# Keys' transposes and first heads one unit later, bias tables ahead of the first product, forget columns in eight pieces

## The chip, the cores and the metric

The kernel runs on one core of a Trainium2 chip. The metric is the time of one execution on the device in microseconds (us), as the median of several runs; the profile shows one execution. The engines are PE (TensorE, matrix products and transposes), DVE (VectorE), ACT (ScalarE), POOL (GpSimd) and SP (SyncE, which here only issues DMAs). Each engine takes its instructions in order.

## The reference, cut to what matters

Two residual layers on x of 256 rows and 1024 columns, all in float32. Each layer normalizes x, multiplies it with one wide input matrix, feeds the columns to two groups of attention heads with a SiLU gate each, and adds the product with an output matrix. The change is in the first layer, with groups A (block-sparse, here plain causal with a linear position bias) and B (forgetting attention).

```python
h = rmsnorm(x, norm_gain[0])
proj = h @ w_in_ab[0]                      # 1024 x 4104
qa, ka, va, ga, qb, kb, vb, gb, fb = split_cols(proj, [512] * 8 + [8])
qa, ka = rmsnorm(heads(qa), moba_q_gain), rmsnorm(heads(ka), moba_k_gain)
s = qa @ ka.T * scale - slope[h] * (t - s) # causal; slope[h] = 2 ** -(h + 1)
ya = softmax(s) @ va
log_f = log_sigmoid(fb + b_forget)         # the last 8 columns, one per head
s = qb @ kb.T * scale + cumsum(log_f)[t] - cumsum(log_f)[s]
yb = softmax(s) @ vb
x = x + concat(ya * silu(ga), yb * silu(gb)) @ w_out_ab[0]
```

## The kernel before, in words

Weights come in tiles of 512 KB. A tile is loaded by SP into one of four raw buffers (`wraws`, L108), then split in two: ACT casts the high part (`whi`, L120) and DVE subtracts it from the raw tile to get the low part (`wlo`, L121), into one of five buffers. A product is then three matmuls (`mm3`, L258 to L260). A raw buffer is free again when `wlo` is done; a buffer of the split parts is free when PE has used the tile. `loads` keeps three tiles ahead of PE.

In the first layer tile n is the n-th in order: 0 to 7 are qa and ka together (one block of 128 rows by 1024 columns each), 8 to 11 va, 12 to 15 qb, 16 to 19 kb (256 columns each and rows of 1 KB, with 4 forget columns copied in by POOL at L105 from the tile `wf`), 20 to 23 vb, 24 to 31 the gates, 32 to 39 the output. Tiles 0 to 3 have raw buffers of their own.

PE's order is the order of the text. It goes by units: `tick` runs one unit's matmuls (mostly one tile, 12 matmuls of 512 columns), then one step of each running generator, latest first, and then lets new tiles be loaded. `qk_heads` is such a generator for query or key columns: squares and sums, inverse root by ACT's tables, a Newton step and the scaled copies, two empty steps apart from that, and then PE's transposes (L377) whose results ACT and DVE bring to SBUF with the gains (`kf` L387, `khi` L394, `klo` L395). The keys of the first product start one unit after the queries (`later`) and use a spare buffer (`room=True`). `values` copies the values out of their two PSUM banks (L404). All PSUM tiles share eight banks. `heads_a` computes scores (L477, L481), softmax, transposes of the probabilities (L509) and the product with the values (L551) of four heads; `play(12, {1: [heads_a(0)], 5: [heads_a(1)]})` starts it at units 1 and 5 of the twelve that hold tiles 12 to 23.

Up to `gain_cols(0)` the order on all engines is written out by hand (`manual_schedule`). Behind it only PE's is; the order on the other engines is made by a planner with costs of its own, which may move an instruction ahead of others that are not yet due.

`biases` fills `mask` and the tables `negA` of the eight heads, 128 x 256 each, from `rel`, and `tri`, which the forgetting heads need. The first four tables are written between the first units, the other four behind the hand-ordered part. `wf` is filled by one DMA on POOL's queue.

Of the kernel before, what the change touches and what calls it, by code (L numbers as in the profile page):

```python
# [12 lines left out]
OP = mybir.AluOpType  # L13
# [4 lines left out]
KT = D // 128  # L18
HD = 64
EPS = 1e-6  # L20
BIG = 1e30
# [8 lines left out]
def trunk_kernel(  # L30
# [6 lines left out]
    nc = tc.nc  # L37
    x, out = x[0], out[0]
    w_ab, wo_ab, w_cd, wo_cd = w_in_ab[0], w_out_ab[0], w_in_cd[0], w_out_cd[0]
# [20 lines left out]
    def xload(t):  # L60
        nc.sync.dma_start(xs[:, t, :], x[t * 128:(t + 1) * 128, :])


    rel = cst.tile([128, 256], F32, name="rel")
# [7 lines left out]
    def params(eng, rows):  # L72
        for i in rows:
            g = gains[i]
            eng.dma_start(
                prow[i:i + 1, :].rearrange("o (r d) -> o r d", r=2),
                bass.AP(tensor=g.tensor, offset=g.offset, ap=[[64, 1], [0, 2], [1, 64]]))
# [17 lines left out]
    wf = cst.tile([128, KT, 8], F32, name="wf")  # L95


    def wraws(parts, nk, n, raw=None):
        if raw is None:
            raw = wraw.tile([128, WF], F32, name="raw")  # L100
        rv = raw[:, 0:nk * n].rearrange("p (k n) -> p k n", k=nk)
        for (c0, src) in parts:
            if isinstance(src, tuple):
                k0, f0 = src
                nc.gpsimd.tensor_copy(rv[:, :, c0:c0 + 4], wf[:, k0:k0 + nk, f0:f0 + 4])  # L105
                continue
            m = src.shape[1]
            last["sp"] = nc.sync.dma_start(rv[:, :, c0:c0 + m],  # L108
                                           src.rearrange("(k p) n -> p k n", p=128))
        return raw  # L110

    def wload(parts, nk, n, raw=None, pieces=1):
# [15 lines left out]
    tiles, wt, units, running = [], [], [], []  # L128
# [38 lines left out]
    def rsqrt_tables(m, shape):  # L167
        tag = "x".join(str(n) for n in shape[1:])
        y = sml.tile(shape, F32, name="rs_y" + tag)
        nc.scalar.activation(y, m, AF.Ln)  # L170
        nc.scalar.activation(y, y, AF.Exp, bias=0.0, scale=-0.5)
        return y
# [21 lines left out]
    def x_transp(t, j):  # L194
        ps = pa.tile([128, 4, 128], F32, name="at", tag="ps")
        for i in range(4):
            k = 4 * j + i
            nc.tensor.transpose(ps[:, i, :], xs[:, t, k * 128:(k + 1) * 128], ident)
        return ps
# [139 lines left out]
    def qk_heads(ps, nh, col, dst, dup=False, room=None):  # L339
        m = sml.tile([128, 2, nh], F32, name=f"qk_m{nh}")  # L340
        for t in range(2):
            sq = scr.tile([128, 512], F32, name="sq", bufs=3)
            nc.scalar.activation(sq[:, 0:nh * HD], ps[t][:, 0:nh * HD], AF.Square)
            nc.vector.tensor_reduce(m[:, t, :],  # L344
                                    sq[:, 0:nh * HD].rearrange("p (h d) -> p h d", d=HD),
                                    axis=AX.X, op=OP.add)
            nc.vector.tensor_scalar(m[:, t, :], m[:, t, :], 1.0 / HD, H["em"][:, t:t + 1],
                                    op0=OP.mult, op1=OP.add)
        yield
        y = rsqrt_tables(m, [128, 2, nh])  # L350
        yield
        r = rsqrt_newton(m, y, [128, 2, nh])
        qns = []
        for t in range(2):
            if room is None:
                qn = scr.tile([128, 512], F32, name="qn", bufs=2)
            else:
                if t == 0:
                    spare = scr.tile([128, 4, 384], F32, name="e", bufs=2).rearrange("p h n -> p (h n)")
                qn = spare[:, t * 512:(t + 1) * 512]  # L360
            qns.append(qn)
            src = ps[t][:, 0:nh * HD].rearrange("p (h d) -> p h d", d=HD)
            rr = r[:, t, :, None].to_broadcast([128, nh, HD])
            if dup:
                qd = qn[:, 0:nh * 128].rearrange("p (h u d) -> p h u d", u=2, d=HD)
                for u in range(2):
                    nc.vector.tensor_tensor(out=qd[:, :, u, :], in0=src, in1=rr, op=OP.mult)
            else:
                nc.vector.tensor_tensor(out=qn[:, 0:nh * HD].rearrange("p (h d) -> p h d", d=HD),
                                        in0=src, in1=rr, op=OP.mult)  # L370
        yield
        yield
        npair = nh if dup else nh // 2
        for t in range(2):
            pt = pa.tile([128, 4, 128], F32, name="at", tag="ps")
            for i in range(npair):
                nc.tensor.transpose(pt[:, i, :], qns[t][:, i * 128:(i + 1) * 128], ident)  # L377
            dst(t, pt[:, 0:npair, :], H["pcol"][:, col:col + 1])
# [295 lines left out]
    mask = cst.tile([128, 256], F32, name="mask")  # L674
    tri = scr.tile([128, 512], F32, name="ytmp", bufs=1)[:, 0:256]
    negA = cst.tile([128, 8, 256], F32, name="negA")

    def biases(heads):
        if 0 in heads:
            nc.vector.tensor_scalar(mask, rel, 0.0, BIG, op0=OP.is_lt, op1=OP.mult)  # L680
        else:
            nc.vector.tensor_scalar(tri, rel, 128.0, None, op0=OP.is_le)
        for h in heads:
            nc.vector.scalar_tensor_tensor(out=negA[:, h, :], in0=rel, scalar=2.0 ** -(h + 1),
                                           in1=mask, op0=OP.mult, op1=OP.add)

    def heads_a(half):
        yield from quad64("a", half, lambda i: i, lambda h: h * 64, H["va"],
                          lambda h: negA[:, 4 * half + h, 128:256], lambda h: negA[:, 4 * half + h, :])
# [167 lines left out]
    with tc.manual_schedule():  # L857
        nc.vector.memset(wz, 0.0)
        raws = []
        for n in ("yth", "ytl"):  # L860
            r = act.tile([128, 2, 1024], F32, name=n)
            raws += [r[:, 0, :], r[:, 1, :]]
        xload(0)
        wraws(*tiles[0], raws[0])
        xload(1)
        for i in range(1, 4):
            wraws(*tiles[i], raws[i])
        nc.gpsimd.iota(rel, pattern=[[-1, 256]], base=128, channel_multiplier=1,
                       allow_small_or_imprecise_dtypes=True)
        nc.vector.tensor_scalar(ident, rel[:, 0:128], 128.0, None, op0=OP.is_equal)  # L870
        nc.vector.memset(prow, 0.0)
        params(nc.gpsimd, (0, 4, 1, 5))
        warm(WARM[0])
        pgt = pv.tile([128, 512], F32, name="av", tag="ps")
        nc.tensor.transpose(pgt[:, 0:16], grow, ident[0:16, 0:16])
        nc.vector.tensor_copy(gcol, pgt[:, 0:16])
        p0 = x_transp(0, 0)
        warm(WARM[1])
        h_block(0, 0, 0, p0[:, 0, :])
        h_block(0, 0, 1, p0[:, 1, :])  # L880
        wt.append(wload(*tiles[0], raws[0], 2))
        mm_first(0, 0, 0)
        p1 = x_transp(1, 0)
        h_block(0, 1, 0, p1[:, 0, :])
        h_block(0, 1, 1, p1[:, 1, :])
        mm_first(0, 0, 1)
        wt.append(wload(*tiles[1], raws[1], 2))
        for j in range(2):
            mm_first(0, 1, j)
        for k in (2, 3):  # L890
            h_block(0, 0, k, p0[:, k, :])
            h_block(0, 1, k, p1[:, k, :])
        run_first(1)
        p0, p1 = x_transp(0, 1), x_transp(1, 1)
        wt.append(wload(*tiles[2], raws[2], 2))
        for k in (4, 5):
            h_block(0, 0, k, p0[:, k - 4, :])
            h_block(0, 1, k, p1[:, k - 4, :])
        run_first(2)
        wt.append(wload(*tiles[3], raws[3], 2))  # L900
        for k in (6, 7):
            h_block(0, 0, k, p0[:, k - 4, :])
            h_block(0, 1, k, p1[:, k - 4, :])
        run_first(3)
        at["freed"] += 3
        loads(3)
        bfor = bcast(nc.gpsimd, "bfor", b_forget, 8)
        nc.gpsimd.dma_start(wf, w_ab[:, 4096:4104].rearrange("(k p) n -> p k n", p=128))
        g = norm_r()
        next(g)  # L910
        running.append(g)
        at["freed"] += 1
        tick(1)
        biases((0, 1, 2, 3))
        tick(3)
        gain_cols(0)

    def play(n, starts):
        for i in range(n):
            for g in starts.get(i, ()):  # L920
                running.append(g)
            tick()

    biases(range(4, 8))
    tick(4)
    play(12, {1: [heads_a(0)], 5: [heads_a(1)]})
    play(12, {0: [heads_b(0)], 3: [heads_b(1)]})
    drain()
    tick(4)
# [50 lines left out]
```

## Time and profile before

| what | value |
|---|---|
| median of 3 runs | 278.92 us |
| lowest and highest run | 276.66 and 279.52 us |
| the profiled execution | 279.85 us |
| its span in the profile | 278.1 us |
| busy in the span: PE, DVE, ACT, POOL | 267.6, 212.2, 178.6, 7.2 us |

The span is the time from the first to the last recorded instruction; what the run takes beyond it lies around the program. Busy time of PE counts a matmul as long as the profile models it, at whatever clock it ran.

### The profile page before, as it was taken

To read this page: it belongs to the slowest core of one execution; us is meant where nothing else is said; L and a number is where in the kernel's file an instruction comes from. 1 tells how busy PE (TensorE), PEld (TensorE's weight loads), DVE (VectorE), ACT (ScalarE), POOL (GpSimd) and SP (SyncE) were. 2 spreads that over 40 slices of the span, in tenths; PEclk is the share of its full clock that TensorE was granted. 3 is DMA by queue.
4 is the path that set the end of the run, shared out by engine and by line. 5 is a ranking of instruction groups with operands and counts; after the bars stand their busy time and mean duration, and the time that the engine had idled before them with its cause. 6 is when DMAs were issued, how large, how long until landed. Compare 5 with 4: busy or idle time off the path is not lost.

```text
span 278.1 us, 4629 instructions
## 1 busy us (share of the span) xinstructions
PE 267.6 (96%) x1665; PEld 225.7 (81%) x1665; DVE 212.2 (76%) x499; ACT 178.6 (64%) x394; POOL 7.2 (3%) x15
## 2 busy tenths in 40 slices
PE   7999999779999999999999999999999999999994
PEld 2876788558998889999788888888987899897784
DVE  2667998287877549999954988776999888698822
ACT  3469572576687557699742845465785798898500
POOL 6000003000000000000000000000000000000000
PEclk9999999979999999999999999999999999999999
DMA  7974864671444472205855367665508125307012
GB/s 238 202 317 128 225 194 150 195 239 24 148 143 116 118 222 78 77 8 165 247 195 165 90 213 242 212 181 182 167 1 272 35 73 175 132 4 222 5 75 76
DMA packets 26297, 41.38 MB, mean 149 GB/s; under 512 B 1665, under 2 KB 13330, under 8 KB 26274
## 3 DMA queue, kind: packets, MB, share of 16 engines
q1 hardware_dynamic: 26050, 41.04, 47.7%
q0 software_dynamic: 192, 0.04, 1.4%
q8 instruction: 13, 0.21, 0.3%
q14 instruction: 10, 0.08, 0.1%
q10 hardware_dynamic: 32, 0.01, 0.0%
HBM read 40.03 MB, written 1.05 MB: 148 GB/s over the span
## 4 chain that ended last, share of the span: by engine, by line
PE 74%; DMA 9%; DVE 8%; ACT 5%; issue 1%; SPq 1%; ACTq 0%
PE pj L258 21%; PE pj L259 20%; PE pj L260 20%; DMA ytl<-in_w_in_ab_dram 5%; DMA raw<-in_w_in_ab_dram 4%; DVE wlo L121 4%; PE at L509 3%; PE av L551 3%; ACT whi L120 2%; PE at L481 2%; PE at L377 2%; PE at L477 1%; DVE qk_m L344 1%; ACT yb L235 1%; DVE klo L395 1%
## 5 line engine op out<-in xcount | busy, mean ns | idle before, releaser
L121 DVE TENSOR_TENSOR wlo<-raw,whi 128x1024 fp32r<-128x1024 f32 (+1 forms) x70 | 85.2, 1223 | 21.8 <-ACT whi L120 18.3
L120 ACT CAST whi<-raw 128x1024 fp32r<-128x1024 f32 (+1 forms) x70 | 72.4, 1048 | 38.0 <-PE pj L259 20.4
L258 PE MATMUL pj<-whi,hth 128*128 128x512 f32 (+2 forms) x192 | 73.7, 384 | 0.6 <-ACT whi L120 0.5
L260 PE MATMUL pj<-wlo,hth 128*128 128x512 f32 (+2 forms) x192 | 71.2, 371 | 0.5 <-DVE wlo L121 0.5
L259 PE MATMUL pj<-whi,htl 128*128 128x512 f32 (+2 forms) x192 | 71.1, 370 | 0.0
L258 PEld LDWEIGHTS pj<-whi,hth 128*128 128x128 f32 x192 | 36.7, 191 | 8.5 <-ACT whi L120 2.0
L260 PEld LDWEIGHTS pj<-wlo,hth 128*128 128x128 f32 x192 | 36.6, 191 | 8.1 <-DVE wlo L121 1.6
L259 PEld LDWEIGHTS pj<-whi,htl 128*128 128x128 f32 x192 | 36.9, 192 | 5.6
L258 PE MATMUL pj<-hth,whi 128*128 128x256 f32 x128 | 37.0, 289 | 0.0
L260 PE MATMUL pj<-htl,whi 128*128 128x256 f32 x128 | 36.0, 281 | 0.0
L259 PE MATMUL pj<-hth,wlo 128*128 128x256 f32 x128 | 35.9, 281 | 0.0
L258 PE MATMUL pj<-whi,yth 128*128 128x512 f32 (+1 forms) x68 | 26.4, 388 | 0.0
L260 PE MATMUL pj<-wlo,yth 128*128 128x512 f32 (+1 forms) x68 | 25.9, 381 | 0.0
L259 PE MATMUL pj<-whi,ytl 128*128 128x512 f32 (+1 forms) x68 | 25.8, 380 | 0.0
L258 PEld LDWEIGHTS pj<-hth,whi 128*128 128x128 f32 x128 | 24.1, 188 | 0.7 <-issue 0.3
L259 PEld LDWEIGHTS pj<-hth,wlo 128*128 128x128 f32 x128 | 24.2, 189 | 0.0
L260 PEld LDWEIGHTS pj<-htl,whi 128*128 128x128 f32 x128 | 24.1, 188 | 0.0
L490 ACT ACTIVATE e<-e,mn 128x128 f32<-128x128 f32 x32 | 12.5, 390 | 8.9 <-DVE mn L486 8.9
L492 ACT ACTIVATE e<-e,mn 128x256 f32<-128x256 f32 x32 | 15.8, 495 | 0.0
L258 PEld LDWEIGHTS pj<-whi,yth 128*128 128x128 f32 x68 | 12.8, 188 | 2.7 <-issue 0.3
L260 PEld LDWEIGHTS pj<-wlo,yth 128*128 128x128 f32 x68 | 12.8, 188 | 2.6
L259 PEld LDWEIGHTS pj<-whi,ytl 128*128 128x128 f32 x68 | 12.8, 188 | 2.5
(167 smaller groups left out, 390.0 us busy)
## 6 DMA issues: line engine op xcount, KB each, us to landing
raw<-in_w_in_ab_dram SPq DMA_DIRECT2D x28, 512.0 KB, 7.9
raw<-in_w_in_cd_dram SPq DMA_DIRECT2D x26, 512.0 KB, 4.5
raw<-in_w_out_ab_dram SPq DMA_DIRECT2D x8, 512.0 KB, 3.7
raw<-in_w_out_cd_dram SPq DMA_DIRECT2D x8, 512.0 KB, 4.6
xs<-in_x_dram SPq DMA_DIRECT2D x2, 512.0 KB, 6.0
yth<-in_w_in_ab_dram SPq DMA_DIRECT2D x2, 512.0 KB, 7.0
ytl<-in_w_in_ab_dram SPq DMA_DIRECT2D x2, 512.0 KB, 12.7
out_dram<-xs SPq DMA_DIRECT2D x3, 256.0 KB, 2.0
```

The source lines that it names most:

```text
L120: last["act"] = nc.scalar.copy(hi[:, c], raw[:, c])
L121: last["dve"] = nc.vector.tensor_tensor(out=lo[:, c], in0=raw[:, c], in1=hi[:, c].bitcast(F32), op=OP.subtract)
L235: nc.scalar.activation(dump, xs[:, t, :], AF.Square, accum_out=ss[:, t:t + 1])
L258: nc.tensor.matmul(ps, ah, bh, start=first, stop=False)
L259: nc.tensor.matmul(ps, al, bh, start=False, stop=False)
L260: nc.tensor.matmul(ps, ah, bl, start=False, stop=last)
L377: nc.tensor.transpose(pt[:, i, :], qns[t][:, i * 128:(i + 1) * 128], ident)
L481: nc.tensor.matmul(scs[b][:, 128:384], q[r[b], i, :], k[r[b], ik, :], start=n == 0, stop=n == 2)
L490: nc.scalar.activation(e[:, 0:128], e[:, 0:128], AF.Exp, bias=mn[:, 0:1], scale=-1.0, accum_out=sm[:, 0:1])
L492: nc.scalar.activation(e[:, 128:384], e[:, 128:384], AF.Exp, bias=mn[:, 1:2], scale=-1.0, accum_out=sm[:, 1:2])
L509: nc.tensor.transpose(pt[:, i * 128:(i + 1) * 128], blocks[j + i], ident)
L551: nc.tensor.matmul(av[64 * b:64 * b + 64, i, t * 128:256], v[:, t, c:c + 64], p, start=t == 0, stop=t == 1)
```

## The change

Four edits. The wait before the transposes in `qk_heads` is one step longer for the keys of the first product, and `heads_a` starts at units 2 and 6 in place of 1 and 5. `mask` and tables 0 to 2 are computed right behind `ident` and the clearing of `prow`, tables 3 to 5 behind `gcol`; tables 6 and 7 and `tri` stay behind the hand-ordered part. The forget columns are loaded by eight DMAs on SP's queue, each of 128 rows of 32 bytes, behind the loads of tiles 8 to 15, and the one DMA on POOL's queue is gone.

```diff
@@ wraws
                                            src.rearrange("(k p) n -> p k n", p=128))
+        k = len(wt) - KT
+        if 0 <= k < KT:
+            nc.sync.dma_start(wf[:, k, :], w_ab[k * 128:(k + 1) * 128, 4096:4104])
         return raw
@@ qk_heads
         yield
         yield
+        if room is not None:
+            yield
         npair = nh if dup else nh // 2
@@ biases
     def biases(heads):
-        if 0 in heads:
-            nc.vector.tensor_scalar(mask, rel, 0.0, BIG, op0=OP.is_lt, op1=OP.mult)
-        else:
-            nc.vector.tensor_scalar(tri, rel, 128.0, None, op0=OP.is_le)
         for h in heads:
@@ the part ordered by hand
         nc.vector.memset(prow, 0.0)
+        nc.vector.tensor_scalar(mask, rel, 0.0, BIG, op0=OP.is_lt, op1=OP.mult)
+        biases((0, 1, 2))
         params(nc.gpsimd, (0, 4, 1, 5))
...
         nc.vector.tensor_copy(gcol, pgt[:, 0:16])
+        biases((3, 4, 5))
         p0 = x_transp(0, 0)
...
         bfor = bcast(nc.gpsimd, "bfor", b_forget, 8)
-        nc.gpsimd.dma_start(wf, w_ab[:, 4096:4104].rearrange("(k p) n -> p k n", p=128))
...
         tick(1)
-        biases((0, 1, 2, 3))
         tick(3)
         gain_cols(0)
@@ behind it
-    biases(range(4, 8))
+    biases((6, 7))
+    nc.vector.tensor_scalar(tri, rel, 128.0, None, op0=OP.is_le)
     tick(4)
-    play(12, {1: [heads_a(0)], 5: [heads_a(1)]})
+    play(12, {2: [heads_a(0)], 6: [heads_a(1)]})
```

## Rows read from the trace of the kernel before

**Rows 1.** The page, part 1: busy us, share of the span, instructions.

```profile
PE 267.6 (96%) x1665; PEld 225.7 (81%) x1665; DVE 212.2 (76%) x499; ACT 178.6 (64%) x394; POOL 7.2 (3%) x15
```

**Rows 2.** Timeline of PE, 46 to 70 us: start, length, what, idle before.

```profile
49.56 0.60 PE L377 MATMUL at<-ident,e 128*128 128x128 f32 x4
52.23 0.66 PE L377 MATMUL at<-ident,e 128*128 128x128 f32 x4 [2.07 <-ACT v L404]
...
56.43 0.49 PE L477 MATMUL at<-kf,qf 64*128 64x128 f32 x4 [0.75 <-ACT kf L387]
...
59.80 0.79 PE L258 MATMUL pj<-whi,hth 128*128 128x512 f32 x1
...
63.75 0.39 PE L258 MATMUL pj<-whi,hth 128*128 128x512 f32 x1
```

**Rows 3.** Windows of PE: length, busy (instructions), granted clock, DMA share, GB/s.

```profile
60.00:62.50 2.50, 2.50 (x7) 0.57 0.73 217
```

**Rows 4.** Timeline of ACT, 50 to 56 us.

```profile
50.53 1.06 ACT L120 CAST whi<-raw 128x1040 fp32r<-128x1040 f32 x1 [4.67 <-DMA raw<-in_w_in_ab_dram]
51.50 0.68 ACT L404 ACTIVATE v<-pj,n_r 128x512 f32<-128x512 f32 x1
...
54.73 1.06 ACT L120 CAST whi<-raw 128x1040 fp32r<-128x1040 f32 x1 [1.39 <-DMA raw<-in_w_in_ab_dram]
55.69 0.68 ACT L387 ACTIVATE kf<-at,pcol 128x512 f32<-128x512 f32 x1
```

**Rows 5.** The raw tile's DMAs issued in 43 to 45 us (tile 18).

```profile
L108 SPq DMA_DIRECT2D raw<-in_w_in_ab_dram x1: 762/762/762, 43.9 to 43.9; - x1
...
DMA to landing us min/median/max: 13.0/13.0/13.0
```

**Rows 6.** Windows of DVE: length, busy (instructions), clock, DMA share, GB/s.

```profile
28.00:44.00 16.00, 15.96 (x34) 1.00 0.73 211
```

**Rows 7.** Line L684: duration ns min/median/max, first and last start us.

```profile
L684 DVE SCALAR_TENSOR_TENSOR negA<-rel,mask x8: 415/418/426, 29.3 to 37.0; 128x256 f32<-128x256 f32 x8
```

**Rows 8.** Timeline of all engines, 0 to 33 us.

```profile
3.76 0.17 DVE L876 COPY gcol<-av 128x16 f32<-128x16 f32 x1 [2.00 <-PE av L875]
...
4.70 0.91 POOL L908 DMA_DIRECT2D wf<-in_w_in_ab_dram  x1
...
14.89 1.04 PE L198 MATMUL at<-ident,xs 128*128 128x128 f32 x8
15.36 1.14 ACT L120 CAST whi<-ytl 128x512 fp32r<-128x512 f32 x2 [1.97 <-DMA ytl<-in_w_in_ab_dram]
...
23.23 0.50 PE L260 MATMUL pj<-wlo,hth 128*128 128x512 f32 x1 [0.53 <-DVE wlo L121]
...
29.34 1.43 DVE L684 SCALAR_TENSOR_TENSOR negA<-rel,mask 128x256 f32<-128x256 f32 x4
...
32.54 1.28 ACT L343 ACTIVATE sq<-pj 128x512 f32<-128x512 f32 x2 [1.22 <-PE pj L260]
```

**Rows 9.** DMA issues by line: count, KB, us to landing.

```profile
wf<-in_w_in_ab_dram POOLq DMA_DIRECT2D x1, 32.0 KB, 10.7
...
sink<-in_swa_sinks_dram SPq DMA_DIRECT2D x1, 4.0 KB, 2.5
```

**Rows 10.** Windows: length, PE, PEld, DVE, ACT, POOL, clock, DMA share, GB/s.

```profile
6.00:9.00 3.00, 2.50 (x8) 1.62 (x7) 1.65 (x3) 1.41 (x3) 0.00 (x0) 1.00 1.03 404
...
10.00:11.50 1.50, 1.50 (x6) 1.13 (x5) 0.91 (x3) 1.23 (x3) 0.00 (x0) 1.00 0.00 0
11.50:14.00 2.50, 2.50 (x13) 2.02 (x12) 2.10 (x6) 1.32 (x5) 0.00 (x0) 1.00 0.41 169
...
34.00:44.00 10.00, 10.00 (x44) 7.88 (x43) 10.00 (x24) 6.28 (x11) 2.58 (x3) 1.00 0.70 209
```

**Rows 11.** Timeline of ACT, 60 to 70 us.

```profile
66.53 1.05 ACT L120 CAST whi<-raw 128x1024 fp32r<-128x1024 f32 x1 [0.60 <-PE pj L259]
```

**Rows 12.** Timeline of ACT, 68 to 105 us.

```profile
87.11 1.56 ACT L511 COPY pT<-at 128x512 f32<-128x512 f32 x3
```

## Prediction

> **What bounds the kernel now.** I read the page first: TensorE (PE) is busy for 267.6 of 278.1 us [rows 1], so what can be won is its idle time, some 10 us, and stretches in which it is busy but slow. Then I read PE's timeline forward and looked for gaps and for the granted clock. Between the start and the tail they lie in one stretch, and idle time of VectorE (DVE), ScalarE (ACT) or the queues elsewhere is not worth a look.
>
> That stretch, 49 to 64 us, reads so [rows 2]. Tile 12 of the weights (the first of the four tiles of the forgetting queries) ends at 49.6, then the four transposes of the first half of the first heads' keys run. The other four need a PSUM bank and start at 52.23, 2.07 us late, released by an ACT copy of values. Tile 13 follows until 55.7. Then the scores of the first heads wait 0.75 us for kf, then again for khi and klo, and tile 14 starts at 59.80. It takes until 63.75, 3.95 us, because PE's granted clock had fallen after these stalls: 0.57 of full speed between 60.0 and 62.5, so mostly its lower level of 1.2 GHz out of 2.4 [rows 3]. The tile before it took 55.68 - 52.23 less 0.6 us for four transposes, about 2.9 us, so the clock costs about 1.1.
>
> Who is late is seen on ACT [rows 4]. ACT takes its instructions in order. The cast of tile 16 sits in its queue between the two copies of values, and waited 4.67 us for that tile's DMA, so the second copy, which frees the bank, came at 51.50. The cast of tile 17 sits ahead of kf and waited 1.39 us more for its DMA, so kf began at 55.69. From kf's start to PE's return at 59.80 it is 4.1 us: kf, khi in two pieces, klo in two, two pairs of scores. So the root is in-order ACT behind DMAs that land late. Tile 18 takes 13.0 us from its issue at 43.9, which puts it at 56.9 [rows 5].
>
> These DMAs are issued when a raw buffer comes free, which is when DVE has finished the tile four before. DVE was busy for 15.96 us of the 16 from 28 to 44 [rows 6], and the bias tables are in there.
>
> **Part 1: the tables leave that stretch.** Eight negA instructions ran between 29.3 and 37.0 [rows 7]; four in a row took 1.43 us, so 0.36 each, about 3 us for all [rows 8]. How much of that moves tiles 16 to 18? The squares of the first queries start at 32.54, released by PE [rows 8], so what DVE saves before them waits for PE. The four tables behind them are on the chain: 4 x 0.36 = 1.4 us. I bound the gain for tiles 15 to 18 by 1.0 (some is lost in waits for casts) and 1.4, plus what the start gives. Tables 6 and 7 and tri now stand outside the hand order: if the planner leaves them where they are written, they take back under 1 us of it, hence the lower bound. The six early tables cost DVE 6 x 0.36 + 0.2 = 2.4 us. Three stand in the gap of 2.00 us ahead of gcol, and three in the one behind it, which ends when ACT delivers the first hth [rows 8]. Their price is nothing while x is on its way; without that cover it would be at most the 2.4.
>
> **Part 2: the forget columns.** The one 32 KB DMA on GpSimd's queue was issued at 4.7 us [rows 8] and landed 10.7 us later, at 15.4 [rows 9]. In the same time the weights stood still: 0 GB/s from 10.0 to 11.5 and 169 from 11.5 to 14.0, against 404 before the hole [rows 10]. Counting lost bytes at 400 GB/s, that is 1.5 us + 2.5 x 0.58 = 2.9, with the edges about 3.5 us of the queue. ACT then waited 1.97 us for tile 2, and PE 0.53 us at 23.23 for tile 4's low part [rows 8]. Without the hole tile 2 is there when ACT is free; but ACT's next h blocks need the transposes of x, which PE does from 14.89 to 15.9 in either case, so not all of the 1.97 us is won. Bounds: PE's own 0.53 and ACT's 1.97. I take 0.9, nearer to PE's row, since that is the engine that counts.
>
> What it adds: eight DMAs of 128 rows of 32 bytes on SP's queue, each behind one of tiles 8 to 15 and so ahead of the next tile. SP's issue is cheap and SP waits for buffers anyway. On the rings the price is not in the trace. From above: a DMA of just that shape, the sinks, took 2.5 us from issue to landing [rows 9], 20 us for eight, though most of it is latency. From below: nothing, since the queue was only 0.70 busy from 34 to 44 [rows 10]. In between, the 3.5 us hole over eight pieces, 0.44 each. I take the 0.44, half of it hidden in the free 0.3, which leaves the lower part of the gain: tiles 16 to 18 land 1.0 to 2.2 us earlier (1.0 to 1.4 of part 1, plus 0 to 0.9 of the start, less the pieces). The wait added is GpSimd's: its copies into tiles 16 and 17 now wait for the pieces. Behind them on GpSimd stands nothing else, and the cast of tile 16 waits until 50.5 for its own DMA, so this is hidden by several us.
>
> The Trainium skill speaks against this part. Its page "DMA: Bandwidth & Descriptors", section "Rules for kernel authors", says to merge small transfers, since below 64 KB one pays mostly overhead, and its section "Bandwidth" has a measured 0.68 us for 4 KB against 0.95 for 64 KB. By that, as an estimate, eight pieces would be 5.4 us of queue in place of under 0.95. This trace agrees for small rows in so far as the 32 KB cost the queue 3.5 us; it doesn't show pieces on SP's queue. The rule bears on the slower rival below.
>
> **Part 3: keys' transposes and heads one unit later.** Nothing is added or removed, but PE now runs tile 13 directly behind tile 12 and has it done at about 52.4, or 51.5 with the 0.9 of the start. The bank for the second four transposes is freed by the copy of values: today 52.2, then 50 to 51. So the 2.07 us stall goes. Transposes 1.2 us, then tile 14, 2.9 us: PE stands before the scores at about 55.6 with tile 14 done.
>
> What is late next? The scores still need kf, and the question is which cast stands ahead of kf on ACT. The trace shows the planner's habit: a tile's cast goes just where its buffer comes free, ahead of the activations that end the same unit. Tile 16 stood between the two value copies, tile 17 ahead of kf [rows 4], tile 20 at 66.53, the moment that PE lets go of tile 15 [rows 11]. There are five buffers, so tile 18's buffer is tile 13's. With the transposes now behind tile 13, tile 18 goes ahead of kf as tile 17 did. Then kf starts when tile 18 has landed (56.9 less 1.0 to 2.2, so 54.7 to 55.9) and is cast (1.06): 55.8 to 57.0. Add the 4.1 us: PE resumes at 59.9 to 61.1. Before, the same work was done at 63.75. That gains 2.65 to 3.85. PE idles again for some 3 us in 5, so the clock may fall again; with even odds, half of 1.1.
>
> The later units shift too. The second heads' 12 transposes now come in the same unit as those of the first forgetting keys, so more banks are wanted at once. The three copies that free theirs took 1.56 us [rows 12]; that is the upper bound, and below there is nothing to win. I take 0.2.
>
> **The sum.** Middle 3.3, less 0.55 for the clock, less 0.2: 2.6 us. The profiled execution took 279.85 us (span 278.1 and 1.75 around it) and would take 277.2; it was 0.9 above the median of the runs, so against the median of 278.92 I forecast 276.3. PE's busy share of 96% [rows 1] leaves little slack behind this stretch, so what is won there should reach the end.
>
> **The rivals.**
> Tile 17 and not 18 gates kf. If the planner places tile 18's cast behind khi, kf waits only for tile 17, which is there by about 53.5, cast by 54.6: PE resumes at 57.6 to 58.8, with little idling and no fall of the clock. Gain 4.9 to 6.1: 272.8 to 274.0. For it: tile 18 stood behind khi before. Against: the habit above.
>
> The gain is eaten. The pieces take back what DVE gives, tile 18 lands at 56.9 as before, PE resumes at 62.05 and the clock falls in full: 63.75 - 63.15 = 0.6: 278.3. For it: tile 18's 13.0 us show how slow this queue can be [rows 5]; against: the free share [rows 10].
>
> Slower: the pieces clog SP's queue. They stand ahead of tiles 9 to 16 in the one queue that feeds everything, and ACT takes what lands in order. Break-even is where PE resumes at 63.75 - 1.1, so tile 18 at 57.5: 1.6 to 2.8 us of delay beyond the cover, 0.2 to 0.35 per piece. With 0.44 each and no cover it would be about 1 us slower; with 1 us each, 8 us later than 55.3 (the middle of 54.7 to 55.9), PE resumes at 68.5, with the clock 5.8 slower: 284.7. I price it at 281.5. The free share of the queue speaks against. The rule of the Trainium skill named above points the same way as this rival.
>
> **How the numbers follow.** Forecast 0.51, tile 17 gating 0.20, eaten 0.17, slower 0.12. The measurement can tell about 1%, 2.8 us, from no change, so faster means below 276.1. Of the forecast (own range 275.1 to 278.4) a little under half lies there, with the first rival: 0.44. Same: the rest of the forecast, the eaten gain and the mild end of slower: 0.44. Slower 0.12. The range 272.9 to 279.4 leaves out the top of the first rival and most of the last.
>
> **What the profile would show.** PE without a gap between tile 12 and the end of tile 14. ACT's order: tile 18's cast ahead of kf, waiting for its DMA. DVE's tables before 6 us. No standstill of the weights at 10 us, and ACT's wait for tile 2 gone. Tiles 16 to 18 issued 1 to 2 us earlier. I am wrong if the ACT order differs, if tiles 9 to 18 land later than before, or if a new PE wait shows at the second heads' transposes.

## The result, and the profile after

The changed kernel takes 274.57 us (median of 4 runs, 273.74 to 275.19), against 279.22 for the kernel before in the same comparison. The ratio is 0.9879 with a 95% interval of 0.9838 to 0.9920. That is 1.2% faster, and the interval leaves out no change. One of the four runs of before, 281.04, fell in a slower state, and the ratio goes by the others; without it the median of before is 278.92 and the difference of the medians 4.35 us, where the ratio makes it 3.4. The forecast was 276.3, with a range of 272.9 to 279.4.

The profiled execution took 273.74 us with a span of 271.9, where that of before took 279.85 and 278.1. These 6.2 us of span are more than the 4.35 us between the medians, in part because the two profiles differ in the clock as well; that is taken apart below.

On the page, part 1 answers to [rows 1]: PE's busy time fell by 3.3 us and the span by 6.2.

```profile
span 271.9 us, 4636 instructions
PE 264.3 (97%) x1665; PEld 223.4 (82%) x1665; DVE 212.1 (78%) x499; ACT 178.2 (66%) x394; POOL 6.3 (2%) x14
```

PE's timeline after, for the start and the middle (start, length, what, idle before). It answers to [rows 2] and, in its first two lines, to [rows 8].

```profile
13.96 1.04 PE L201 MATMUL at<-ident,xs 128*128 128x128 f32 x8
21.19 0.50 PE L263 MATMUL pj<-wlo,hth 128*128 128x512 f32 x1
...
50.30 1.04 PE L382 MATMUL at<-ident,e 128*128 128x128 f32 x8
...
54.49 0.49 PE L482 MATMUL at<-kf,qf 64*128 64x128 f32 x4 [0.38 <-ACT kf L392]
55.65 0.39 PE L486 MATMUL at<-khi,qhi 64*128 64x256 f32 x2 [0.67 <-ACT khi L399]
...
56.52 0.38 PE L486 MATMUL at<-klo,qhi 64*128 64x256 f32 x2 [0.36 <-DVE klo L400]
...
57.41 0.50 PE L261 MATMUL pj<-whi,hth 128*128 128x512 f32 x1
...
82.73 1.47 PE L514 MATMUL at<-ident,e 128*128 128x128 f32 x12
```

The reader is to see four things. The low part of tile 4 starts 2.04 us earlier (21.19 for 23.23) and no longer waits. The eight transposes of the keys run in one piece without the stall of 2.07 us. The waits at the scores are still there: 0.38, 0.67 and 0.36 us. And at 57.41 PE starts tile 15, which began at 63.75 before: 6.34 us earlier, about as much as the whole span won (6.2). So nearly all that happened lies ahead of this point.

ACT's timeline after, in the same two stretches; it answers to [rows 8] and [rows 4].

```profile
12.91 1.13 ACT L123 CAST whi<-ytl 128x512 fp32r<-128x512 f32 x2
14.59 1.59 ACT L224 ACTIVATE hth<-at,gcol 128x128 fp32r<-128x128 f32 x4 [0.55 <-PE at L201]
...
18.84 1.98 ACT L123 CAST whi<-raw 128x1024 fp32r<-128x1024 f32 x2
...
46.13 1.06 ACT L123 CAST whi<-raw 128x1040 fp32r<-128x1040 f32 x1 [2.77 <-DMA raw<-in_w_in_ab_dram]
47.09 0.68 ACT L409 ACTIVATE v<-pj,n_r 128x512 f32<-128x512 f32 x1
...
49.80 1.06 ACT L123 CAST whi<-raw 128x1040 fp32r<-128x1040 f32 x1 [0.87 <-DMA raw<-in_w_in_ab_dram]
52.80 1.06 ACT L123 CAST whi<-raw 128x1040 fp32r<-128x1040 f32 x1 [1.93 <-DMA raw<-in_w_in_ab_dram]
53.76 0.68 ACT L392 ACTIVATE kf<-at,pcol 128x512 f32<-128x512 f32 x1
```

The cast of tile 2 at 12.91 waits for no DMA, where it waited 1.97 us; behind it ACT waits 0.55 us for PE's transposes of x. The cast of tile 16 runs at 46.13 and so the copy of values behind it at 47.09, 4.4 us earlier than before and ahead of the transposes that need its bank. Then two casts, of tiles 17 and 18, wait for their DMAs ahead of kf: the order that the prediction named, 2 us and more ahead of its times.

The weights no longer stand still. Windows of after (length, busy of PE, PEld, DVE, ACT, POOL, PE clock, DMA share, GB/s), for the 0 and 169 GB/s of [rows 10]:

```profile
10.00:11.50 1.50, 1.50 (x8) 1.14 (x7) 1.05 (x3) 1.50 (x5) 0.00 (x0) 1.00 1.12 273
11.50:14.00 2.50, 2.50 (x13) 1.98 (x12) 2.17 (x6) 1.92 (x6) 0.00 (x0) 1.00 0.93 310
```

DVE's timeline after shows where the tables went. Eight of them are done before 6.8 us, since the planner moved the last two forward as well:

```profile
1.89 1.08 DVE L685 SCALAR_TENSOR_TENSOR negA<-rel,mask 128x256 f32<-128x256 f32 x3
...
6.00 0.75 DVE L685 SCALAR_TENSOR_TENSOR negA<-rel,mask 128x256 f32<-128x256 f32 x2
```

The DMA issues of the forget columns (first and last start) show that the planner did the same to the pieces: the first was issued at 7.6 us. Five were issued by 14.3 us, and only three later, from 21.6 to 26.4.

```profile
L112 SPq DMA_DIRECT2D wf<-in_w_in_ab_dram x8: 328/328/470, 7.6 to 26.4; - x8
```

The issue of tile 18, for [rows 5]: 3.2 us earlier and 1.0 us shorter, so the tile lands at 52.7, 4.2 us earlier.

```profile
L108 SPq DMA_DIRECT2D raw<-in_w_in_ab_dram x1: 368/368/368, 40.7 to 40.7; - x1
...
DMA to landing us min/median/max: 12.0/12.0/12.0
```

### The profile page after: what moved, and what is told of

Same layout as the page of the kernel before. It is cut to its first block, busy times and chain, and to the rows that moved or that the text cites. A ratio compares the mean times of both kernels' runs of the same rounds, so it can differ in the third digit from the quotient of the medians.

```text
span 271.9 us, 4636 instructions
## 1 busy us (share of the span) xinstructions
PE 264.3 (97%) x1665; PEld 223.4 (82%) x1665; DVE 212.1 (78%) x499; ACT 178.2 (66%) x394; POOL 6.3 (2%) x14
## 4 chain that ended last, share of the span: by engine, by line
PE 78%; DMA 10%; DVE 5%; ACT 3%; issue 1%; SPq 1%; ACTq 0%
PE pj L261 22%; PE pj L263 21%; PE pj L262 21%; DMA raw<-in_w_in_ab_dram 8%; PE at L514 3%; PE av L556 3%; DVE wlo L124 2%; PE at L486 2%; PE at L382 2%; DMA wf<-in_w_in_ab_dram 2%; PE at L482 1%; ACT whi L123 1%; DVE qk_m L347 1%; DVE klo L400 1%; ACT e L497 1%
## 5 line engine op out<-in xcount | busy, mean ns | idle before, releaser
L124 DVE TENSOR_TENSOR wlo<-raw,whi 128x1024 fp32r<-128x1024 f32 (+1 forms) x70 | 85.2, 1222 | 20.6 <-ACT whi L123 14.3
L261 PE MATMUL pj<-whi,hth 128*128 128x512 f32 (+2 forms) x192 | 72.4, 377 | 0.5 <-ACT whi L123 0.5
L262 PEld LDWEIGHTS pj<-whi,htl 128*128 128x128 f32 x192 | 36.3, 189 | 5.8 <-DVE htl L225 0.2
L261 PE MATMUL pj<-whi,yth 128*128 128x512 f32 (+1 forms) x68 | 26.4, 388 | 0.0
```

The lines of the kernel that those rows point to most:

```text
L124: last["dve"] = nc.vector.tensor_tensor(out=lo[:, c], in0=raw[:, c], in1=hi[:, c].bitcast(F32), op=OP.subtract)
L261: nc.tensor.matmul(ps, ah, bh, start=first, stop=False)
L262: nc.tensor.matmul(ps, al, bh, start=False, stop=False)
```

## The experiments

Three questions were open after this. Which part gives what? Does kf, with the cast of tile 18 ahead of it, hold what is left? And why did the weights stand still: because of the 1024 rows of 32 bytes, as I had put it, or because the DMA was on GpSimd's queue? Every ratio below is against the kernel before on the same chip.

| kernel | median us (runs) | ratio, 95% | first matmul behind the scores, and its tile |
|---|---|---|---|
| part 3 alone | 279.88 (10) | 1.0071, 1.0041 to 1.0101 | 61.50, tile 15 |
| part 1 alone | 276.15 (10) | 0.9942, 0.9907 to 0.9977 | 56.84, tile 14 |
| part 2 alone | 276.45 (10) | 0.9937, 0.9902 to 0.9971 | 56.49, tile 14 |
| parts 1 and 3 | 276.44 (10) | 0.9944, 0.9908 to 0.9980 | 60.09, tile 15 |
| parts 1 and 2 | 274.76 (6) | 0.9868, 0.9827 to 0.9910 | 55.46, tile 14 |
| the change, again | 275.01 (6) | 0.9882, 0.9842 to 0.9923 | 57.74, tile 15 |
| pieces in order | 275.44 (10) | 0.9898, 0.9865 to 0.9930 | 57.76, tile 15 |
| one DMA on SP | 275.87 (10) | 0.9912, 0.9876 to 0.9949 | 59.11, tile 15 |
| tile 18 behind khi | 273.69 (6) | 0.9861, 0.9808 to 0.9913 | 55.43, tile 15 |
| the same, again | 272.98 (6) | 0.9804, 0.9755 to 0.9853 | 55.72, tile 15 |
| parts 1 and 2, tile 17 behind khi | 273.20 (6) | 0.9820, 0.9783 to 0.9856 | 53.04, tile 14 |
| part 3 and idle matmuls | 278.68 (12) | 1.0013, 0.9982 to 1.0044 | 61.00, tile 15 |

A tile at full clock takes PE 2.9 us, so a time for tile 14 is compared with one for tile 15 by adding that.

### Part 3 alone

```diff
+        if room is not None:
+            yield
...
-    play(12, {1: [heads_a(0)], 5: [heads_a(1)]})
+    play(12, {2: [heads_a(0)], 6: [heads_a(1)]})
```

> The kernel before with part 3 alone (keys' transposes and heads one unit later). My theory, one chain in which each part releases another wait: PE has no gap up to the end of tile 14 (about 56 us), then waits for kf, which stands behind the cast of tile 18; that lands at about 56.9 as before, so kf starts near 58.0, PE resumes near 62.1 in place of 63.75: 1.6 us faster at equal clock, 0.5 if the clock falls. Rival, the move of the transposes is the whole change: 5 to 6 us faster in the profile and kf no later than 56.

The order came as expected, with kf at 57.17 and PE back at 61.50, both somewhat ahead of the expected times. The time did not: 0.7% slower. PE's timeline of this run, and the windows that show its clock:

```profile
57.90 0.49 PE L479 MATMUL at<-kf,qf 64*128 64x128 f32 x4 [1.83 <-ACT kf L389]
...
61.50 0.79 PE L258 MATMUL pj<-whi,hth 128*128 128x512 f32 x1
...
66.50 0.29 PE L258 MATMUL pj<-whi,hth 128*128 128x260 f32 x1
```

```profile
60.00:64.00 4.00, 4.00 (x18) 3.29 (x19) 3.45 (x17) 2.53 (x11) 0.00 (x0) 0.50 0.76 223
64.00:68.00 4.00, 4.00 (x21) 3.44 (x20) 2.16 (x5) 2.87 (x9) 0.00 (x0) 0.73 0.08 29
```

PE has tile 14 done when it waits, and starts tile 15 at 61.50 in place of 63.75. Then the granted clock is 0.50 for all of 60 to 64, its lower level, so tile 15 takes 5.0 us. Tile 16, whose first matmul is the one of 260 columns, starts at 66.50. In the trace of before it starts here:

```profile
66.52 0.28 PE L258 MATMUL pj<-whi,hth 128*128 128x260 f32 x1
```

So in these two profiles the 2.25 us of order were paid back to the last tenth by the clock. They take the same time (279.96 and 279.85 us); the 0.7% are against all runs of the kernel before, of which about half are without a fall of the clock. The stall did not go away; it moved from the transposes into one wait of 1.83 us at the scores, behind which the clock fell for longer than in the kernel before, where the waits of 2.07 and 0.75 us lie some 4 us apart [rows 2, 3]. The mean granted clock of the execution was 0.985 to 0.987 in 9 of 10 runs of this kernel; the kernel before has 0.992 or more in nearly all.

### Part 1 alone, part 2 alone

```diff
+        nc.vector.tensor_scalar(mask, rel, 0.0, BIG, op0=OP.is_lt, op1=OP.mult)
+        biases((0, 1, 2))
...
+        biases((3, 4, 5))
...
-        biases((0, 1, 2, 3))
...
-    biases(range(4, 8))
+    biases((6, 7))
+    nc.vector.tensor_scalar(tri, rel, 128.0, None, op0=OP.is_le)
```

> The kernel before with part 1 alone (bias tables early). My theory: tiles 15 to 18 are issued 1.0 to 1.4 us earlier, the stall at the keys' transposes and kf move by as much, PE gains about 1.2 us and the clock may still fall. The start is unchanged (PE's wait at 23.2 us stays). Rival, DVE is what bounds the stretch: 3 us, the whole of the tables' time.

```diff
+        k = len(wt) - KT
+        if 0 <= k < KT:
+            nc.sync.dma_start(wf[:, k, :], w_ab[k * 128:(k + 1) * 128, 4096:4104])
...
-        nc.gpsimd.dma_start(wf, w_ab[:, 4096:4104].rearrange("(k p) n -> p k n", p=128))
```

> The kernel before with part 2 alone (forget columns in eight pieces on SP's queue). My theory: no standstill of the weights at 10 us, the low part of tile 4 and everything up to 45 us about 2.0 us earlier, as in the changed kernel, and the stalls at 50 to 60 us keep their length: 2.0 us faster. Rival, the start is hidden behind the later DMA-bound stretch: the stalls grow by what the start wins, under 0.5 us in all.

Each is faster by 0.6% by itself. Part 1 was to give 1.2 us and gave about 1.6; part 2 was to give 2.0 and gave about 1.7. PE's timeline of part 1 alone, its cast of tile 16 on ACT, and the time from issue to landing of that tile's DMA, first in the kernel before, then in this one:

```profile
49.55 1.03 PE L377 MATMUL at<-ident,e 128*128 128x128 f32 x8
...
56.84 0.50 PE L258 MATMUL pj<-whi,hth 128*128 128x512 f32 x1
```

```profile
48.30 1.07 ACT L120 CAST whi<-raw 128x1040 fp32r<-128x1040 f32 x1 [2.90 <-DMA raw<-in_w_in_ab_dram]
```

```profile
raw<-in_w_in_ab_dram SPq DMA_DIRECT2D x1, 512.0 KB, 9.1
...
raw<-in_w_in_ab_dram SPq DMA_DIRECT2D x1, 512.0 KB, 8.2
```

PE's timeline of part 2 alone:

```profile
47.93 0.60 PE L380 MATMUL at<-ident,e 128*128 128x128 f32 x4
49.61 0.66 PE L380 MATMUL at<-ident,e 128*128 128x128 f32 x4 [1.08 <-ACT v L407]
...
56.49 0.50 PE L261 MATMUL pj<-whi,hth 128*128 128x512 f32 x1
```

With part 1 the start is unchanged (the transposes ahead of tile 12 stand at 45.90, before at 45.92), but the cast of tile 16 runs at 48.30 for 50.53 [rows 4], 2.2 us earlier, and the stall of 2.07 us [rows 2] is gone, though the transposes stand where they stood. Of the 2.2 us, 1.27 are an earlier issue (40.04 for 41.31), within the 1.0 to 1.4 that were expected; the rest is the shorter way from issue to landing. With part 2 the start gains 1.6 us and the stall is halved, to 1.08, where it was expected to keep its length. Neither needs part 3 for this: the bank is late because the cast ahead of the copy of values waits for a DMA, and whatever brings that DMA forward shortens the wait.

### Parts 1 and 3, parts 1 and 2

The first is the changed kernel without part 2, the second without part 3.

```diff
-        k = len(wt) - KT
-        if 0 <= k < KT:
-            nc.sync.dma_start(wf[:, k, :], w_ab[k * 128:(k + 1) * 128, 4096:4104])
...
+        nc.gpsimd.dma_start(wf, w_ab[:, 4096:4104].rearrange("(k p) n -> p k n", p=128))
```

> The changed kernel without part 2 (forget columns again by one DMA on GpSimd's queue). My theory: the standstill at 10 us and PE's wait at 23.2 us are back, tile 18 lands about 55.5, kf starts at about 56.5, PE resumes at about 60.7: 2 to 3 us slower than the changed kernel, 3 us faster than before. Rival, part 2 does nothing by itself: as fast as the changed kernel within 0.7 us.

```diff
-        if room is not None:
-            yield
...
-    play(12, {2: [heads_a(0)], 6: [heads_a(1)]})
+    play(12, {1: [heads_a(0)], 5: [heads_a(1)]})
```

> The changed kernel without part 3 (transposes and heads as early as before). With parts 1 and 2 tile 16 is cast at 47.2, so the bank for the keys' transposes is free before PE wants it at 47.9, and kf, now behind tile 17's cast (50.9) again, starts at about 50.9. My theory, that part 3 has nothing left to win once the DMAs land earlier: scores wait about 1.3 us behind tile 13, PE resumes at 55.0 and starts tile 15 at 57.8, within 0.5 us of the changed kernel's 57.41. Rival, part 3 is what makes the other two pay: 2 us or more slower than the changed kernel.

Parts 1 and 3 give what part 1 gives alone (0.9944 and 0.9942); the standstill at 10 us is back. Parts 1 and 2 give what the whole change gives (0.9868 and 0.9879). PE's timeline of parts 1 and 2:

```profile
47.92 1.03 PE L380 MATMUL at<-ident,e 128*128 128x128 f32 x8
...
52.54 0.49 PE L480 MATMUL at<-kf,qf 64*128 64x128 f32 x4 [0.80 <-ACT kf L390]
...
55.46 0.50 PE L261 MATMUL pj<-whi,hth 128*128 128x512 f32 x1
```

There is no stall at the transposes here either. Tile 15 follows at 58.35, 0.9 us behind the changed kernel's profile, but the medians show no such difference, and why is open. So, as far as these runs can tell (about 0.4%), part 3 is worth nothing once parts 1 and 2 are there, and alone it costs.

### The cast of tile 18 behind khi

```diff
-            last["act"] = nc.scalar.copy(hi[:, c], raw[:, c])
+            with ExitStack() as es:
+                if len(wt) == 18:
+                    es.enter_context(tc.issue_after(last_khi["khi"].ins))
+                last["act"] = nc.scalar.copy(hi[:, c], raw[:, c])
```

`last_khi` holds the last khi copy of the first keys.

> The changed kernel with one edge more: ACT's cast of tile 18 is issued behind the last khi, so that kf waits for no DMA. My theory, that this cast alone gates the scores: kf starts at about 50.9 instead of 53.76, the scores start right behind tile 14 at 54.1, PE resumes at 55.5 instead of 57.41, 1.9 us faster than the changed kernel. Rival, another wait takes its place (the cast of tile 18 or 19 now late for the softmax that follows on ACT, or for its own unit): the 1.9 us are given back before 70 us.

ACT's timeline of this run, and PE's:

```profile
51.22 0.68 ACT L395 ACTIVATE kf<-at,pcol 128x512 f32<-128x512 f32 x1
...
53.34 1.06 ACT L126 CAST whi<-raw 128x1040 fp32r<-128x1040 f32 x1 [0.28 <-DMA raw<-in_w_in_ab_dram]
```

```profile
54.08 0.49 PE L487 MATMUL at<-kf,qf 64*128 64x128 f32 x4
...
55.43 0.50 PE L264 MATMUL pj<-whi,hth 128*128 128x512 f32 x1
```

kf starts at 51.22 for 53.76, the scores wait for nothing, and tile 15 starts 1.98 us earlier than in the changed kernel. The tile itself is cast only 0.54 us later (53.34 for 52.80) and nobody waits for it. So the cast ahead of kf did hold what was left. Not all of it reaches the end: the expectation's rival, a wait that takes its place, holds for a part. PE starts tile 18 only 1.41 us earlier (65.85 for 67.26), behind a new wait of 0.35 us for DVE ahead of the transposes of the probabilities, and the spans differ by 1.3 us (270.6 and 271.9).

In the runs the kernel is 0.9 to 2.0 us faster than the changed one (273.69 and 272.98, against 274.57 and 275.01). A part of that is the clock, which falls in 2 of its 12 runs and in 6 of 10 of the changed kernel. Where it doesn't fall, the medians are 273.33 (10 runs) and 273.94 (4), 0.6 us apart. The intervals of the ratios overlap, so the size is not settled. A second run of both, on two chips:

> The changed kernel once more, beside the others of this call: 0.985 to 0.99 of the time before; in executions without a fall of the clock kf starts at 53.8 and PE resumes at 57.4.

> The changed kernel with tile 18's cast behind the last khi, once more with more runs: PE resumes at 55.4 instead of 57.4, and the median is 1 to 2 us below the changed kernel's.

The second profile of the changed kernel has the same order and another clock:

```profile
57.74 0.79 PE L261 MATMUL pj<-whi,hth 128*128 128x512 f32 x1
```

```profile
56.00:60.00 4.00, 3.84 (x18) 3.22 (x19) 3.57 (x18) 2.48 (x11) 0.00 (x0) 0.57 0.69 195
```

### Parts 1 and 2 with the cast of tile 17 behind khi

The kernel with parts 1 and 2 and the edge above, with `len(wt) == 17`.

> Parts 1 and 2 and not 3, and ACT's cast of tile 17 behind the last khi. kf then starts right behind the keys' transposes, at about 49.0, and khi and klo are done about when tile 13 ends at 51.7. My theory: no wait over 0.4 us at the scores, tile 15 starts at about 55.6, as in the changed kernel with kf ahead of tile 18's cast (55.43). Rival, a later cast of tile 17 holds up ACT's softmax or tile 17 itself: tile 15 not before 57.

PE's timeline:

```profile
51.69 0.49 PE L485 MATMUL at<-kf,qf 64*128 64x128 f32 x4
...
53.04 0.50 PE L264 MATMUL pj<-whi,hth 128*128 128x512 f32 x1
```

No wait at the scores, and tile 15 follows at 55.9, close to the 55.43 with part 3. The time, 273.20, is that of the run above as well. Two new small waits show later, 0.62 us for mn (what the softmax subtracts from each row) at the products with the values, and 0.21 us for qn at tile 18. This and the kernel above are the two fastest; which of them is faster can't be told.

### One DMA on SP's queue

The pieces are replaced by the old DMA of 32 KB, issued from SP.

```diff
-        k = len(wt) - KT
-        if 0 <= k < KT:
-            nc.sync.dma_start(wf[:, k, :], w_ab[k * 128:(k + 1) * 128, 4096:4104])
...
+        nc.sync.dma_start(wf, w_ab[:, 4096:4104].rearrange("(k p) n -> p k n", p=128))
```

> The changed kernel with the forget columns in one 32 KB DMA of 1024 rows of 32 bytes, as before the change, but on SP's queue, where the planner puts it ahead of the load of tile 6. My theory, that 1024 small rows at once cost the rings 3 us wherever they come from: a standstill of the weights of about 3 us is back, now a little earlier, tile 2 or 4 late and 1 to 2 us slower than the changed kernel. Rival, that GpSimd's queue makes the standstill: no standstill, as fast as the changed kernel within 0.7 us, and then the pieces are not needed.

Windows of this run, at the time of the former standstill and later:

```profile
10.00:11.00 1.00, 1.00 (x6) 0.78 (x6) 0.56 (x2) 0.70 (x2) 0.00 (x0) 1.00 1.02 311
...
14.00:16.00 2.00, 2.00 (x14) 1.76 (x13) 1.68 (x4) 1.29 (x4) 0.00 (x0) 1.00 0.51 144
```

The packets of this run in 14 to 16 us, and the same window of the changed kernel:

```profile
DMA packets 751, 0.29 MB, mean 144 GB/s; under 512 B 686, under 2 KB 686, under 8 KB 751
```

```profile
14.00:16.00 2.00, 2.00 (x15) 1.78 (x14) 1.77 (x5) 1.31 (x5) 0.00 (x0) 1.00 1.04 360
```

The same 1024 rows, in one DMA, and the weights never stand still. But they do slow down, only later: though this DMA is issued at 4.9 us, its rows are sent as small packets, most of them from 13 to 18 us. There the rate is 144 and then 185 GB/s, where the changed kernel has 360 and 263. Counted against 400 GB/s as in the prediction, that is 2.4 us of queue from 14 to 18 us (0.9 in the changed kernel), an estimate. So my theory of the small rows fell as the cause of the standstill, and not as a price. By then ACT has tile 2, whose cast starts at 13.32 without a wait, and PE loses little: the low part of tile 4 starts at 21.68, in the changed kernel at 21.19 and before at 23.23.

What makes the standstill in the kernel before is seen in the packets by queue. In 9 to 10 us (packets, MB, share of the 16 DMA engines; a packet is counted whole by its start, so the share can pass 100%):

```profile
q0 software_dynamic: 16, 0.03, 379.1%
q1 hardware_dynamic: 40, 0.13, 31.3%
```

GpSimd's queue (software) sent the 1024 rows as 16 packets of 2 KB, and a packet held its engine for 3.79 x 16 / 16 = 3.8 us on average. Meanwhile SP's queue (hardware) got nothing: from 10.0 to 11.5 us no packet of any queue begins. The Trainium skill, "DMA: Bandwidth & Descriptors", section "Queues, rings and completion order", says that an engine changes between queues only at the end of a packet; the trace agrees. How much of the gain comes from the other queue and how much from the later time of the rows, no run separates.

The single DMA still costs: its first cast of tile 4 is at 19.33 us, 0.5 behind the changed kernel. So for the eight pieces the runs speak against the rule of merging small transfers that the prediction weighed: merged into one on the same queue they give 275.87, in pieces 274.57 and 275.01, so they are not slower. The two figures of the Trainium skill that the prediction worked its 5.4 us from, in "DMA: Bandwidth & Descriptors", section "Bandwidth", are for DMAs issued from GpSimd, so they did not price pieces on SP's queue.

### All eight pieces in line

To test the rival that pieces clog SP's queue, they were held in the order of the text; only the first three were left to the planner.

```diff
+            with tc.issue_after(last["sp"].ins) if k > 2 else ExitStack():
+                nc.sync.dma_start(wf[:, k, :], w_ab[k * 128:(k + 1) * 128, 4096:4104])
```

> The changed kernel with every one of the eight pieces held behind its tile on SP's queue (in the changed kernel the planner issues five of them between tiles 7 and 8, when the rings are busy with the first tiles). My theory, that a piece costs the queue about 0.3 us: the first tiles land up to 1 us earlier, tiles 12 to 16 up to 1 us later, kf within 0.7 us of 53.8, the same time within 0.7 us. Rival, a piece holds up the tile behind it by 1 us or more each: tile 18 lands after 56, PE resumes after 60, 2 us slower or more.

kf starts at 53.64 (53.76 in the changed kernel) and PE resumes at 57.76, with a fall of the clock as in the second run of the change (57.74). The ratio, 0.9898, lies within the intervals of the changed kernel. The pieces cost nothing that can be seen, wherever they stand.

### Part 3 with idle matmuls in the wait

This isolates the clock: part 3 alone, with eight matmuls on data of no use between tile 14 and the scores, so that PE works while it waits for kf.

```diff
+        if half == 0:
+            pt, wk = bank(), rel.bitcast(BF16)
+            for _ in range(8):
+                nc.tensor.matmul(pt, wk[:, 0:128], wk, start=True, stop=True)
```

> Part 3 alone with eight idle matmuls (128x512 in bf16, into a bank of their own, results unused) between tile 14 and the scores, where PE stood still for 1.83 us. My theory, that part 3 alone lost because one longer gap brought the clock down, for 5.5 us of half speed: with the gap filled the clock stays at 1.00, PE resumes at 61.5 again, tile 15 takes 2.8 us and the kernel is 2 to 2.5 us faster than part 3 alone. Rival, the lower clock comes from something else and stays: no faster than part 3 alone.

```profile
56.27 1.68 PE L693 MATMUL pj<-rel 128*128 128x512 bf16 x7
...
61.00 0.50 PE L258 MATMUL pj<-whi,hth 128*128 128x512 f32 x1
```

The trace holds seven of the eight. PE resumes at about the same place as with part 3 alone (61.00 for 61.50), now at full clock: the first matmul takes 0.50 us for 0.79. The median is 1.2 us better than part 3 alone. I had expected 2 to 2.5; the clock still falls in half of the runs (6 of 12 have a mean granted clock of 0.994 or less), so the account by the clock is confirmed in kind and only half in size. Nor is it the whole account: the six runs without a fall have a median of 278.11, and those of the kernel before 277.36, so part 3 with the wait filled gains nothing even at full clock. Where its 2.25 us go then is not shown, since the only profile of the kernel before is one with a fall.

### What the clock does to the comparison

Executions of one kernel differ in whether the clock falls in this stretch, and that shows in the mean granted clock of each. Medians by that clock:

| kernel | 0.997 and more: us (runs) | below: us (runs) |
|---|---|---|
| before | 277.36 (38) | 278.90 (42) |
| the change, both comparisons | 273.94 (4) | 275.14 (6) |
| part 1 alone | 275.74 (6) | 277.41 (4) |
| part 2 alone | 275.16 (4) | 276.96 (6) |
| parts 1 and 3 | 276.11 (6) | 277.59 (4) |
| parts 1 and 2 | 273.76 (3) | 275.83 (3) |
| part 3 alone | none | 279.88 (10) |

The clock is worth 1.2 to 2.1 us, and at the same clock the change is worth 3.4 us (277.36 less 273.94) to 3.8. Parts 1 and 2 add up: 1.6 and 2.2 alone, 3.6 together. The profile of before was an execution with a fall of the clock and that of after one without, which is why their spans lie 6.2 us apart.

## Why the prediction was right, and where it was not

The sign and the range held, and the mechanism in the middle was the forecast's. The sum was too small: 2.6 us of gain, where the medians show 4.35, and the ratio and the runs at equal clock 3.4 to 3.8. That it was not further off is in part luck, since terms that were too low (the start, the landing) stood beside a part 3 that was credited with an effect it doesn't have.

**The start was sized too low.** The term was 0.9 us, between PE's own 0.53 and ACT's 1.97, taken nearer to PE's row. It measured 2.04, beyond the upper bound, and 1.6 with part 2 alone; what adds the rest no run isolates. The step that failed is that PE does the transposes of x from 14.89 "in either case": they came at 13.96, so they held ACT for only 0.55 us. PE's own wait of 0.53 was the end of a chain that had been late all along, and I took the last wait for the size of the delay.

**The cause of the standstill was wrong, though the step worked.** I laid the 3.5 us to the small rows, and from that came 0.44 for each piece, half of it hidden. The run with one DMA on SP shows no standstill with the same rows, though they still slow the weights down later. What stopped the weights altogether was 16 packets of 3.8 us from GpSimd's queue. The pieces cost no time that the runs show, so what I took off for them was taken off for nothing.

**Part 1 gave more than its instructions.** I had 1.0 to 1.4 us, four tables of 0.36. Alone, it brings tile 16's cast forward by 2.2 and ends the stall. The issue moves by 1.27, as forecast; the other 1.0 is a way from issue to landing of 8.2 us for 9.1. Why that is shorter is not settled; with idle matmuls and without part 1 it was 8.6, so a part of it is spread between executions. That the planner might leave tables 6 and 7 in the stretch, my lower bound, did not happen.

**The landing of tile 18** moved by 4.2 us, where 1.0 to 2.2 was forecast. Of the 3.2 by which it is issued earlier, 2.04 are the start and 1.2 the tables, and 1.0 is a shorter landing (12.0 for 13.0), for which I had no term. Most of this 1.0 is spread between executions as far as the runs show: part 3 alone, and the same with idle matmuls, issue the tile at 43.8 and 43.9 us as before, and in both it lands after 12.3.

```profile
raw<-in_w_in_ab_dram SPq DMA_DIRECT2D x1, 512.0 KB, 12.3
```

**The order on ACT** was right: tile 18's cast ahead of kf, waiting for its DMA. Hence kf at 53.76, not at 55.8 to 57.0, and PE at 57.41, not at 59.9 to 61.1, the same chain shifted by the landing. From kf to PE it took 3.65 us, not 4.1, since the 4.1 of [rows 4] and [rows 2] held half-clock matmuls.

**Part 3 was credited with what the other two do.** The step "so the 2.07 us stall goes" is right as a row of the trace and wrong as a cause. Part 1 alone ends the stall, part 2 alone halves it, and part 3 alone moves it to the scores, where it costs more. I never asked what each part would do without the others; a chain with one late DMA behind two waits has only one gain to give.

**The clock** had a term of 0.55, half of 1.1. The fall comes in 42 of 80 runs of the kernel before and in 6 of 10 of the changed one, and costs 1.5 and 1.2 us. So with these few runs it is no difference between the two, and the 1.1 of the profile of before should not have stood in a comparison of medians at all, on either side.

**The second heads' transposes** had 0.2 us. They run at 82.73 without a wait. From tile 16 to the end the changed kernel takes 211.67 us and the kernel before 211.54, so it is 0.1 at most.

In the two profiles the 6.34 us are then: 2.04 of the start, 2.07 of the stall, 0.37 of the wait for kf (0.75 less 0.38), about 1.1 of the clock in tile 14 and 0.45 of it between kf and PE, and 0.3 left over, in part since the eight transposes run as one group. That is 4.8 without the clock, while the runs at equal clock give 3.4 to 3.8. The profile of before was 0.95 above the median of its kind and that of after 0.2 below, which is about the difference; the late landing of tile 18 in the profile of before may be a part of it.

**The rivals.** Tile 17 gating kf was to give 272.8 to 274.0. Its times came near by another way; its mechanism did not happen by itself, and where it was made to, it gave 273.69 and 272.98, with PE back at 55.43, ahead of the 57.6 to 58.8 forecast, as the landings were earlier too. The eaten gain and the clogged queue did not happen: the pieces in line cost nothing that can be seen. The slower side existed, but in a place where I had not looked for it: part 3 alone.

## What to carry to other kernels

When several edits shorten one chain, price each alone and in pairs before adding: here two of three did all the work that the runs can tell, and the third, alone, made the kernel slower. A wait that is gathered into one place can cost more than the same wait spread out: here the clock fell for longer behind it. And look for a cast that waits for a DMA ahead of the copy that PE wants, in an engine that takes its work in order: one edge that sets the copy first gave another 0.9 to 2.0 us in the medians, 0.6 where the clock doesn't fall.

## What the runs showed of the hardware that was not expected

A 32 KB DMA of 1024 rows on GpSimd's queue went as 16 packets, each of which held its DMA engine for 3.8 us on average, and the loads on SP's queue stood at 0 GB/s for 1.5 us. Issued from SP, the same rows went as small packets between the weights and left the queue at 144 to 185 GB/s from 14 to 18 us, without a standstill.

PE's clock, granted at half behind a wait of 1.83 us at the scores, stayed there for the whole of 60 to 64 us and cost tile 15 some 2 us, as much as the order had won in these two profiles. It falls in about half of the executions of the kernel before, and in the profiles that show a fall it lies at the scores or behind them, so that medians of few runs carry a difference of 1.2 to 1.5 us that has nothing to do with the edit.
